# A two-layer hybrid backbone on Trainium2: the 32x32 inverses of the gated DeltaNet laid out by VectorE transposes instead of DMA, with other fill amounts and buffers

## The chip, the cores and the metric

One core of one Trainium2 chip runs the kernel. The metric is the device time of one execution in microseconds; smaller is better. A profiled execution gives the trace that the rows below come from.

## The reference, cut to what matters

The model has two layers over 512 latent tokens and 256 context tokens, 1024 wide. A layer normalises and modulates the stream, projects it once, and feeds three parallel mixers: a Conformer convolution, a neighbourhood attention, and a bidirectional gated DeltaNet (GDN). Their outputs are merged through sigmoid gates, and a gated ConvFFN follows. The change is in the GDN. Per head, direction and chunk of 64 tokens it solves a unit lower triangular system:

```python
lmat = jnp.where(strict, jnp.einsum("bhnid,bhnjd->bhnij", kb, k) * decay, 0.0)
rhs = jnp.concatenate([v * beta, kb * jnp.exp(g)[..., None]], axis=-1)
sol = lax.linalg.triangular_solve(lmat, rhs, left_side=True, lower=True, unit_diagonal=True)
```

The GDN has four heads of width 128. The kernel solves by the explicit inverse of blocks of 128 tokens, and needs four rounds of inverses in all: two layers times two pairs of heads. The text calls them L0/0, L0/1, L1/0 and L1/1.

## The kernel before

**Fills.** The GDN core is a long chain of small steps that would leave TensorE idle. So independent work is kept in a queue of generators (neighbourhood-attention projections `na`, convolution projections `pjl` and `pjc`, merge gates), and `fill(us)` (L426) issues as many of its matmuls as a nominal time asks for. The table `FILL` (L33) gives the amounts at each place of the core. A scheduler then places all instructions on the engines' queues; it may move fill matmuls ahead of steps that stand earlier in the code, and each engine runs its queue in order. What the core does not use up of the queue is issued later in the layer.

**Weight units.** Each queued projection loads a 128x1024 weight block on SP's queue into `raw`, ScalarE casts it to `whi` (L131), VectorE subtracts `wlo<-raw,whi` (L132), and TensorE multiplies with `whi` and `wlo` in turn. So a TensorE matmul that needs a `wlo` waits for whatever stands ahead of that subtraction on VectorE.

**The core.** `gdn_core` (L884) makes, for each of two heads and two directions, a decay `D` (VectorE L900, ScalarE exponential L902), products `kk` and `qk` on TensorE, and from them `E` (L912) and `A` (L924) on VectorE. Then it calls `gdn_inverse`, loads keys and values (`tk`) and runs the state chain, which begins with `ch` (L965).

**The inverse.** `gdn_inverse` (L1021) inverts 24 blocks of 128x128 with 32x32 diagonal blocks. It writes the diagonal blocks of `E` to DRAM and reads them back so that a block lies along one partition (L1031 to L1035; 48 partitions for each direction, the second one reversed by a copy). 31 substitution steps of two VectorE operations each follow (L1041, L1043), on 112 partitions. `fill(sub)` stands behind them. Two ScalarE copies and one VectorE copy arrange the result (L1046 to L1048), DMAs write it to DRAM (L1050, L1051), and eight loads bring it back with a block's rows along partitions: `Td`, and the diagonal of `E` (L1058, L1059). TensorE then builds the off-diagonal 32x32 products, `iy` (L1069, 48 matmuls) and `it` and `ir` (L1080, L1082, 72 matmuls), and the 64x64 products `iy` (L1101) and `ir` (L1110), with copies out of PSUM by ScalarE and VectorE between them and the fills `y32`, `t32`, `y64` and `t64`. A trace shows each of these small matmuls as two records. The tiles `D`, `Eb`, `Tt`, `Tf` and the key loads `tk` share a ring of three buffers.

**Convolution taps.** After marked instructions (`self.marks`) the scheduler may start the taps `ca` (L519) of the convolution on VectorE; they are many and short, and fill VectorE's gaps.

Of the kernel before, what the change touches and what calls it, by code (L numbers as in the profile page):

```python
# [9 lines left out]
F32 = mybir.dt.float32  # L10
# [54 lines left out]
class Net:  # L65
# [277 lines left out]
    def layer(self, l):  # L343
# [540 lines left out]
    def gdn_core(self, pr):  # L884
# [6 lines left out]
        for hh in range(2):  # L891
            h = 2 * pr + hh
            Ds = []
            for d in range(2):
                D = gp.tile([128, 1024], F32, tag="D", name="D", bufs=3)[:, 0:768].rearrange("p (t c) -> p t c", c=128)
                r0 = 24 * d + 6 * h
                nc.sync.dma_start(D.rearrange("p t c -> p (t c)"),
                                  self.d_row[r0:r0 + 6].rearrange("a b -> (a b)").unsqueeze(0).to_broadcast([128, 768]))
                for t in range(6):
                    V.scalar_tensor_tensor(D[:, t, :], D[:, t, :], self.G[:, 4 * d + h, t:t + 1], mk[d],  # L900
                                           ALU.subtract, ALU.min)
                S.activation(D, D, AF.Exp)  # L902
                Ds.append(D)
            for t0, t1 in ((2, 6), (0, 2)):
# [17 lines left out]
                for d in range(2):  # L922
# [4 lines left out]
        self.gdn_inverse(E)  # L927

        tk = [gp.tile([128, 1024], F32, tag="D", name=f"tk{i}", bufs=3) for i in range(3)]
# [67 lines left out]
        for hh in range(2):  # L997
            h = 2 * pr + hh
            o = oa[hh]
            sg = gp.tile([128, 6, 128], F32, tag=("Td", "TA")[hh], name="sgr")  # L1000
# [20 lines left out]
    def gdn_inverse(self, E):  # L1021

        nc, V, S, T, gp = self.nc, self.nc.vector, self.nc.scalar, self.nc.tensor, self.gp
        de, dt, dR = self.d_e
        Eb = gp.tile([128, 1024], F32, tag="D", name="Eb", bufs=3)
        Tt = gp.tile([128, 1024], F32, tag="D", name="Tt", bufs=3)
        Tf = gp.tile([128, 1024], F32, tag="D", name="Tf", bufs=3)
        Tm = gp.tile([128, 768], F32, tag="Y", name="Tm")
        nc.gpsimd.memset(Eb[32:64], 0.0)
# [6 lines left out]
        Mv = Eb.rearrange("p (j i) -> p j i", i=32)  # L1036
        Tv = Tt.rearrange("p (i c) -> p i c", c=32)
        for j in range(31):
            n, m = 31 - j, j + 1
            tm = Tm[0:112, 0:n * m].rearrange("p (a b) -> p a b", b=m)  # L1040
            V.tensor_tensor(tm, Mv[0:112, j, j + 1:32].unsqueeze(2).to_broadcast([112, n, m]),  # L1041
                            Tv[0:112, j, 0:m].unsqueeze(1).to_broadcast([112, n, m]), ALU.mult)
            i = V.tensor_tensor(Tv[0:112, j + 1:32, 0:m], Tv[0:112, j + 1:32, 0:m], tm, ALU.subtract)  # L1043
        self.marks.append(i.ins)
        self.fill(FILL[self.l]["sub"])
        S.copy(Mv[0:48], Tv[0:48].rearrange("p i c -> p c i"))  # L1046
        S.copy(Mv[64:112], Tv[64:112].rearrange("p i c -> p c i")[:, ::-1, ::-1])
        V.tensor_copy(Tf[64:112], Tt[64:112, ::-1])  # L1048
        for d, (Rs, Ts) in enumerate(((Eb[0:48], Tt[0:48]), (Eb[64:112], Tf[64:112]))):
            nc.sync.dma_start(dR[:, 12 * d:12 * d + 12, :], Rs)  # L1050
            nc.sync.dma_start(dt[:, 12 * d:12 * d + 12, :], Ts)  # L1051
        Td = gp.tile([128, 24, 32], F32, tag="Td", name="Td")
        TA = gp.tile([128, 12, 64], F32, tag="TA", name="TA")
        nc.gpsimd.memset(TA, 0.0)
        for b in range(4):
            q = slice(32 * b, 32 * b + 32)
            d = b // 2
# [17 lines left out]
        tb, rb = self.bank("it"), self.bank("ir")
        for u in range(12):
            for d in range(2):
                for s, t in prs[d]:
                    if s // 2 == d:
                        T.matmul(tb[32 * t:32 * t + 32, 32 * u:32 * u + 32], blk(t, 12 * d + u, t), Yq(t, u),  # L1080
                                 start=True, stop=True)
                    T.matmul(rb[32 * s:32 * s + 32, 32 * u:32 * u + 32], Yq(t, u), blk(t, 12 * d + u, t),  # L1082
                             start=True, stop=True)
        self.fill(FILL[self.l]["t32"])
        v = lambda x: x.rearrange("p (u c) -> p u c", c=32)
        S.copy(TA[32:64, :, 0:32], v(tb[32:64, 0:384]))
        S.copy(TA[64:96, :, 32:64], v(tb[64:96, 0:384]))
        for d in range(2):
            for s, t in prs[d]:
                V.tensor_copy(E[32 * s:32 * s + 32, 12 * d:12 * d + 12, 32 * t:32 * t + 32], v(rb[32 * s:32 * s + 32, 0:384]))  # L1090
# [4 lines left out]
        ybs, rbs = [], []  # L1095
        for hh in range(2):
            yb = self.bank("iy2")
            for u in range(6 * hh, 6 * hh + 6):
                for d in range(2):
                    s, t = st(d)  # L1100
                    T.matmul(yb[t, 64 * (u - 6 * hh):64 * (u - 6 * hh) + 64], E[s, 12 * d + u, t], TA[s, u, :],  # L1101
                             start=True, stop=True)
            S.activation(Y2[:, 6 * hh:6 * hh + 6, :], w(yb[:, 0:384]), AF.Copy, scale=-1.0)
        self.fill(FILL[self.l]["y64"])
        for hh in range(2):
            rb = self.bank("ir2")
            for u in range(6 * hh, 6 * hh + 6):
                for d in range(2):
                    s, t = st(d)
                    T.matmul(rb[s, 64 * (u - 6 * hh):64 * (u - 6 * hh) + 64], Y2[t, u, :], E[t, 12 * d + u, t],  # L1110
                             start=True, stop=True)
# [430 lines left out]
```

## Time and profile before

| | us |
|---|---|
| median of 3 runs | 2592.03 |
| lowest and highest of them | 2590.8, 2603.91 |
| the profiled execution | 2597.05 |
| its span in the trace | 2595.3 |
| TensorE busy | 2492.7 |
| VectorE busy | 1851.3 |
| ScalarE busy | 1067.5 |
| GpSimd busy | 8.4 |

The profiled execution is 1.75 us longer than its span and 5.0 us above the median. The mean granted clock of TensorE over the span is 0.984 of full speed. TensorE is busy for 96% of the span, so its queue sets the end: idle time of TensorE, and time in which it runs at the lower clock, are what an edit can add or take away, so long as the number of matmuls stays the same.

### The profile page before, as it was taken

Reading aid. Unit: us, or ns where it says so; the run is one execution under the profiler, and the core shown is the slowest. Engines: PE = TensorE matmul, PEld = TensorE weight load, DVE = VectorE, ACT = ScalarE, POOL = GpSimd, SP = SyncE. Lnnn points to the kernel's source line nnn. Section 1 sums busy time; section 2 is a strip of 40 time slices with the busy share of each in tenths; the row PEclk is TensorE's granted clock in tenths of the full one; section 3 lists DMA queues with packets and bytes.
Section 4 is the critical chain, followed back from the end, with each engine's and each line's share of the span. In section 5 each row is a group of like instructions: output and inputs, shape, how many; then the busy total and the mean of one; then the engine's idle time right before and its main releaser. Section 6 shows DMA issues by size and latency. Waiting matters only on the chain. (4 is left out here: it accounts for less than half of the span.)

```text
span 2595.3 us, 42261 instructions
## 1 busy us (share of the span) xinstructions
PE 2492.7 (96%) x16079; PEld 2156.4 (83%) x16079; DVE 1851.3 (71%) x4138; ACT 1067.5 (41%) x2159; POOL 8.4 (0%) x32
## 2 busy tenths in 40 slices
PE   6999999989999999999999999998989999999999
PEld 4889898977778888888888898887877778888887
DVE  6676478789678988776656477776768977755463
ACT  4564342445332344223223345634344543533242
POOL 0000000000000000000000000000000000000000
PEclk9999999999999999999999989998999999999999
DMA  7224434253458553443442342343446375333332
GB/s 253 91 76 138 130 98 142 94 186 107 153 184 267 182 173 123 123 159 116 147 135 87 110 142 96 120 135 112 147 124 213 101 245 188 128 93 98 97 98 89
DMA packets 207275, 356.75 MB, mean 137 GB/s; under 512 B 54832, under 2 KB 103200, under 8 KB 206944
## 3 DMA queue, kind: packets, MB, share of 16 engines
q1 hardware_dynamic: 182176, 320.97, 39.2%
q10 hardware_dynamic: 24896, 33.09, 3.6%
q8 instruction: 126, 2.06, 0.3%
q14 instruction: 77, 0.63, 0.1%
HBM read 297.31 MB, written 56.68 MB: 136 GB/s over the span
## 5 line engine op out<-in xcount | busy, mean ns | idle before, releaser
L132 DVE TENSOR_TENSOR wlo<-raw,whi 128x1024 fp32r<-128x1024 f32 (+2 forms) x319 | 385.4, 1209 | 295.2 <-ACT whi L131 291.8
L131 ACT CAST whi<-raw 128x1024 fp32r<-128x1024 f32 (+2 forms) x319 | 331.9, 1041 | 619.5 <-PE dn L150 198.3
L150 PE MATMUL upl<-hl,whi 128*128 128x512 f32 (+1 forms) x728 | 281.2, 388 | 3.9 <-ACT whi L131 2.3
L150 PE MATMUL upl<-hl,wlo 128*128 128x512 f32 (+1 forms) x728 | 281.0, 387 | 0.2 <-DVE wlo L132 0.2
L150 PE MATMUL upl<-ol,whi 128*128 128x512 f32 (+1 forms) x728 | 281.0, 387 | 0.0
L519 DVE SCALAR_TENSOR_TENSOR ca<-yp,caw,ca 128x783 f32<-128x783 f32 (+1 forms) x240 | 213.0, 888 | 6.4 <-ACT ca L512 3.7
L448 PE MATMUL pjl<-hl,whi 128*128 128x512 f32 x512 | 209.4, 409 | 7.6 <-ACT whi L131 7.6
L448 PE MATMUL pjl<-hl,wlo 128*128 128x512 f32 x512 | 205.5, 402 | 0.8 <-DVE wlo L132 0.7
L448 PE MATMUL pjl<-ol,whi 128*128 128x512 f32 x512 | 205.5, 401 | 0.0
L150 PEld LDWEIGHTS upl<-hl,whi 128*128 128x128 f32 x728 | 136.7, 188 | 33.1 <-ACT whi L131 2.5
L150 PEld LDWEIGHTS upl<-hl,wlo 128*128 128x128 f32 x728 | 136.7, 188 | 29.4 <-DVE wlo L132 0.4
L150 PEld LDWEIGHTS upl<-ol,whi 128*128 128x128 f32 x728 | 136.7, 188 | 29.4
L150 PE MATMUL dn<-fhl,whi 128*128 128x512 f32 x352 | 138.6, 395 | 0.6 <-DVE xml L1406 0.6
L150 PE MATMUL dn<-fll,whi 128*128 128x512 f32 x352 | 139.0, 395 | 0.0
L150 PE MATMUL dn<-fhl,wlo 128*128 128x512 f32 x352 | 139.0, 395 | 0.0
L448 PEld LDWEIGHTS pjl<-hl,whi 128*128 128x128 f32 x512 | 97.4, 190 | 29.0 <-ACT whi L131 9.7
L448 PEld LDWEIGHTS pjl<-hl,wlo 128*128 128x128 f32 x512 | 97.1, 190 | 21.0 <-DVE wlo L132 1.4
L245 DVE CUSTOM_DVE_ANT_1 aj<-at,crows,par 128x512 f32<-128x512 f32 x128 | 93.1, 747 | 29.5 <-DMA at<-ada_t 18.3
L448 PEld LDWEIGHTS pjl<-ol,whi 128*128 128x128 f32 x512 | 97.5, 190 | 19.0 <-issue 0.5
L584 PE MATMUL na<-wlo,hl 128*128 128x256 f32 x384 | 109.6, 285 | 0.6 <-DVE wlo L132 0.6
L584 PE MATMUL na<-whi,hl 128*128 128x256 f32 x384 | 109.8, 286 | 0.0
L584 PE MATMUL na<-whi,ol 128*128 128x256 f32 x384 | 109.8, 286 | 0.0
(405 smaller groups left out, 6457.5 us busy)
## 6 DMA issues: line engine op xcount, KB each, us to landing
raw<-w_b SPq DMA_DIRECT2D x88, 512.0 KB
raw<-f_up SPq DMA_DIRECT2D x88, 512.0 KB
at<-ada_t SPq DMA_DIRECT2D x160, 256.0 KB
raw<-w_o SPq DMA_DIRECT2D x32, 512.0 KB
raw<-f_dn SPq DMA_DIRECT2D x32, 448.0 KB
raw<-w_a SPq DMA_DIRECT2D x24, 512.0 KB
mg<-mge ACTq DMA_DIRECT2D x48, 256.0 KB
raw<-w_br SPq DMA_DIRECT2D x24, 512.0 KB
```

The source lines that it names most:

```text
L131: self.nc.scalar.copy(hi[:, :n], r[:, :n])
L132: self.split = self.nc.vector.tensor_sub(lo[:, :n], r[:, :n], hi[:, :n]).ins
L150: self.nc.tensor.matmul(o, wk[a], x[k][b], start=(k == 0 and i == 0), stop=(k == n - 1 and i == 2))
L245: V.tensor_tensor_reduce(p, w, self.crows[:, r, 4 * h:4 * h + 4], 1.0, m if h else self.p(l, "adab")[:, t:t + 1], ALU.mult, ALU.add, accum ...
L448: self.nc.tensor.matmul(o, wk[a], x[k][b], start=(k == 0 and i == 0), stop=(k == n - 1 and i == 2))
L519: nc.vector.scalar_tensor_tensor(a, y[:, k:k + n], w[:, 31 * c + k:31 * c + k + 1], a, ALU.mult, ALU.add)
L584: self.nc.tensor.matmul(ps[:, :256], x[k][a], wk[b], start=(k == 0 and j == 0), stop=(k == 7 and j == 2))
```

## The change

1. The four inverses no longer go through DRAM. VectorE transposes 32x32 squares instead: the diagonal squares of `E` go into `Db` (second direction by VectorE transposes, first direction by ScalarE copies), `Z` is the transpose of `Db`, the substitution runs on `Z` and `W` on 128 partitions, and two more transposes give `X` and `Yt`. GpSimd sets `W` to the identity.
2. The 32x32 products read `X` and `Yt` directly, with a step of 32 elements, and the copies into `TA` (ScalarE) and into the diagonal of `E` (VectorE) read them with the same step.
3. Each stage of products is cut into two halves of six blocks. `behind()` keeps a half in its place on TensorE's queue, and `wait()` puts a fill of 0.9 between halves.
4. `FILL`: `sub` goes from 37.6 to 47 and 34 (first and second pair of layer 0) and from 38.3 to 50 and 36 (layer 1); `y32`, `t32` and `y64` go.
5. The ring of `D` has five buffers; the new tiles and the key loads `tk` share it. `sgr` gets a buffer of its own in place of `Td`'s.

```diff
-FILL = (dict(e=3.5, sub=37.6, y32=1.6, t32=2.5, y64=1.3, t64=1.0, ...),
-        dict(e=4.1, sub=38.3, y32=1.0, t32=2.5, y64=1.69, t64=1.7, ...))
+FILL = (dict(e=3.5, sub=(47.0, 34.0), inv=0.9, t64=1.0, ...),
+        dict(e=4.1, sub=(50.0, 36.0), inv=0.9, t64=1.7, ...))
...
+    def behind(self):
+        eng = self.nc.tensor.engine
+        last = next((i for i in reversed(self.nc.cur_bb.bb.instructions) if i.engine == eng), None)
+        return self.tc.issue_after(last) if last is not None else ExitStack()
...
-        for b in range(4):
-            nc.sync.dma_start(de[b].rearrange("u (j i) -> j u i", i=32), E[32 * b:32 * b + 32, :, 32 * b:32 * b + 32])
-        nc.sync.dma_start(Eb[0:48], de[:, 0:12, :])
-        nc.sync.dma_start(Tf[64:112], de[:, 12:24, :])
-        V.tensor_copy(Eb[64:112], Tf[64:112, ::-1])
-        nc.sync.dma_start(Tt[0:112], self.A["eye32"][0:112])
+        nc.gpsimd.memset(cube(Db)[:, :, 24:32], 0.0)
+        nc.gpsimd.memset(W, 0.0)
+        nc.gpsimd.memset(W[:, ::33], 1.0)
+        for q in qs:
+            V.transpose(cube(Db)[q, :, 12:24].rearrange("p i u -> p u i"), E[q, 12:24, q])
+            S.copy(cube(Db)[q, :, 0:12].rearrange("p i u -> p u i"), E[q, 0:12, q])
+        V.transpose(Z, Db)
...
-            V.tensor_tensor(tm, Mv[0:112, j, j + 1:32].unsqueeze(2).to_broadcast([112, n, m]),
+            V.tensor_tensor(tm, Zv[:, j + 1:32, j].unsqueeze(2).to_broadcast([128, n, m]),
...
-        self.fill(FILL[self.l]["sub"])
...
-            nc.sync.dma_start(Td[q], dt[b].rearrange("u (j i) -> j u i", i=32))
-            nc.sync.dma_start(E[q, :, q], dR[b].rearrange("u (j i) -> j u i", i=32))
-            S.copy(TA[q, :, 32 * (b % 2):32 * (b % 2) + 32], Td[q, 12 * d:12 * d + 12, :])
+        self.fill(FILL[self.l]["sub"][pr])
+        X, Yt = sq("X"), sq("Yt")
+        V.transpose(X, W)
+        V.transpose(cube(Yt), Wv.rearrange("p i c -> p c i"))
+        inv, ivt = (cube(Yt), cube(X)), (cube(X), cube(Yt))
...
+        for u0, u1 in halves:
+            yb = self.bank("iy")
+            with self.behind():
...
+                            T.matmul(yb[32 * t:32 * t + 32, 32 * (u - u0):32 * (u - u0) + 32], blk(s, 12 * d + u, t),
+                                     inv[d][qs[s], :, 12 * d + u], start=True, stop=True)
+            S.activation(Y1[:, 32 * u0:32 * u1], yb[:, 0:192], AF.Copy, scale=-1.0)
+            wait()
+        for b, q in enumerate(qs):
+            d = b // 2
+            S.copy(TA[q, :, 32 * (b % 2):32 * (b % 2) + 32], inv[d][q, :, 12 * d:12 * d + 12].rearrange("p i u -> p u i"))
+            for d in range(2):
+                us = slice(12 * d, 12 * d + 12)
+                V.tensor_copy(E[q, us, q], ivt[d][q, :, us].rearrange("p i u -> p u i"))
```

The next two listings are VectorE's queue in L0/0, around the end of `E` and `A`, of before and then of the changed kernel. `nrm` is a small reduction of an `na` unit; the `wlo` is that of the first projection `pjl` behind the last `qk`.

```order
L900 SCALAR_TENSOR_TENSOR D<-D,G,km 128x128 x6
L592 TENSOR_REDUCE nrm<-nsq 128x4 x2
L132 TENSOR_TENSOR wlo<-raw,whi 128x1024
L900 SCALAR_TENSOR_TENSOR D<-D,G,km 128x128 x6
L912 SCALAR_TENSOR_TENSOR E<-kk,beta,D 128x128 x8
L924 TENSOR_TENSOR A<-qk,D 128x512 x2
L912 SCALAR_TENSOR_TENSOR E<-kk,beta,D 128x128 x4
L924 TENSOR_TENSOR A<-qk,D 128x256 x2
L592 TENSOR_REDUCE nrm<-nsq 128x4 x2
L132 TENSOR_TENSOR wlo<-raw,whi 128x1024
```

```order
L917 SCALAR_TENSOR_TENSOR E<-kk,beta,D 128x128 x8
L929 TENSOR_TENSOR A<-qk,D 128x512 x2
L917 SCALAR_TENSOR_TENSOR E<-kk,beta,D 128x128 x4
L929 TENSOR_TENSOR A<-qk,D 128x256 x2
L1040 STREAM_TRANSPOSE Db<-E 32x12x32 x4
L597 TENSOR_REDUCE nrm<-nsq 128x4
L1042 STREAM_TRANSPOSE Z<-Db 128x1024
L597 TENSOR_REDUCE nrm<-nsq 128x4
L1047 TENSOR_TENSOR Tm<-Z,W 128x31
L597 TENSOR_REDUCE nrm<-nsq 128x4
L1049 TENSOR_TENSOR W<-W,Tm 128x31
L132 TENSOR_TENSOR wlo<-raw,whi 128x1024
```

The subtraction `wlo` stood between the two groups of `D`; in the changed kernel the twelve `D` operations run together, and it stands behind `E`, `A`, five transposes and the first substitution step.

On the same engine in L1/0, the place that answers to it, before and then after; here the `wlo` belongs to an `na` unit.

```order
L900 SCALAR_TENSOR_TENSOR D<-D,G,km 128x128 x6
L592 TENSOR_REDUCE nrm<-nsq 128x4
L132 TENSOR_TENSOR wlo<-raw,whi 128x1024
L900 SCALAR_TENSOR_TENSOR D<-D,G,km 128x128 x6
L912 SCALAR_TENSOR_TENSOR E<-kk,beta,D 128x128 x8
```

```order
L917 SCALAR_TENSOR_TENSOR E<-kk,beta,D 128x128 x8
L929 TENSOR_TENSOR A<-qk,D 128x512 x2
L917 SCALAR_TENSOR_TENSOR E<-kk,beta,D 128x128 x4
L597 TENSOR_REDUCE nrm<-nsq 128x4
L1040 STREAM_TRANSPOSE Db<-E 32x12x32 x4
L132 TENSOR_TENSOR wlo<-raw,whi 128x1024
```

It has moved in the same way, behind `E` and four transposes.

VectorE's queue in L0/0 at the end of the substitution, before and then after. The copies `E<-ir` are those out of PSUM between the 32x32 and the 64x64 products.

```order
L1043 TENSOR_TENSOR Tt<-Tt,Tm 112x31
L1048 COPY Tf<-Tt 48x1024
L132 TENSOR_TENSOR wlo<-raw,whi 128x1024 x2
L592 TENSOR_REDUCE nrm<-nsq 128x4 x6
L1090 COPY E<-ir 32x12x32 x4
```

```order
L1053 STREAM_TRANSPOSE X<-W 128x1024
L132 TENSOR_TENSOR wlo<-raw,whi 128x1024
L1054 STREAM_TRANSPOSE Yt<-W 128x1024
L1089 COPY E<-X 32x12x32
L1089 COPY E<-Yt 32x12x32
...
L1089 COPY E<-Yt 32x12x32
L132 TENSOR_TENSOR wlo<-raw,whi 128x1024
L493 SCALAR_TENSOR_TENSOR th<-th,pjl 128x512
L493 SCALAR_TENSOR_TENSOR th<-th,pjc 128x256
L132 TENSOR_TENSOR wlo<-raw,whi 128x1024
L1105 COPY E<-ir 32x6x32 x8
```

Eight copies with strided reads now stand ahead of the `wlo` of the last projection that TensorE runs before its first `iy`. On TensorE's queue the work between the last `qk` and the first `iy` of L0/0 was 66.3 us by the pace of its matmuls in the trace (0.119 us from one `na` to the next, 0.236 for a `pjl`, 0.117 for a `pjc`); now it is 76 `na`, 96 `pjl` and 96 `pjc`, which is 42.9 us. In L0/1, L1/0 and L1/1 it goes from 65.4, 60.0 and 64.8 us to 39.2, 48.2 and 45.0 us.

## Rows read from the trace of the kernel before

**Rows 1.** The page, busy us of an engine (share of the span), instructions.

```profile
PE 2492.7 (96%) x16079; PEld 2156.4 (83%) x16079; DVE 1851.3 (71%) x4138; ACT 1067.5 (41%) x2159; POOL 8.4 (0%) x32
```

**Rows 2.** Waits of PE, whole span: what for, us in total, times, longest.

```profile
PE iy L1069 <- DMA Td<-e: 11.6, 5, 4.2
PE pjl L448 <- ACT whi L131: 7.6, 5, 2.6
PE it L1080 <- issue: 4.0, 1, 4.0
PE ir L1082 <- issue: 3.4, 3, 1.7
PE iy L1069 <- issue: 2.2, 1, 2.2
```

**Rows 3.** Four stretches: length, busy of PE, PEld, DVE, ACT, POOL, PE clock, DMA.

```profile
230.00:325.00 95.00, 89.76 (x910) 82.63 (x908) 48.89 (x118) 32.16 (x57) 0.00 (x0) 0.98 0.45 134
376.00:462.00 86.00, 78.63 (x809) 72.85 (x807) 66.71 (x138) 27.05 (x45) 0.00 (x0) 0.92 0.45 129
1690.00:1776.00 86.00, 72.15 (x771) 66.72 (x769) 56.03 (x129) 30.72 (x54) 0.95 (x1) 0.88 0.52 151
1827.00:1917.00 90.00, 82.75 (x726) 70.93 (x724) 58.03 (x123) 29.08 (x43) 0.15 (x2) 0.96 0.52 155
```

**Rows 4.** The same view of stretches at the lower clock inside them.

```profile
301.60:305.00 3.40, 3.40 (x19) 3.40 (x18) 0.00 (x0) 0.34 (x1) 0.00 (x0) 0.51 0.78 150
...
451.80:462.00 10.20, 6.37 (x159) 6.26 (x159) 5.01 (x8) 3.48 (x8) 0.00 (x0) 0.50 0.36 117
...
1759.10:1776.20 17.10, 10.19 (x337) 9.38 (x338) 3.48 (x7) 6.76 (x14) 0.00 (x0) 0.50 0.70 193
```

**Rows 5.** Timeline of DVE, L0/0: start, us, operation, count, idle before.

```profile
230.82 1.21 DVE L132 TENSOR_TENSOR wlo<-raw,whi 128x1024 fp32r<-128x1024 f32 x1
...
238.35 0.75 DVE L924 TENSOR_TENSOR A<-qk,D 128x256 f32<-128x256 f32 x2
239.01 0.73 DVE L592 TENSOR_REDUCE nrm<-nsq 128x4 f32<-128x256 f32 x2
```

**Rows 6.** Timeline of PE, L0/0: last qk, then the first use of that wlo.

```profile
229.36 0.60 PE L920 MATMUL qk<-qT,kT 128*128 128x128 f32 x4
...
233.87 0.40 PE L448 MATMUL pjl<-hl,wlo 128*128 128x512 f32 x1
```

**Rows 7.** Timeline of DVE, L1/0: the wlo, and the last E.

```profile
1691.93 1.22 DVE L132 TENSOR_TENSOR wlo<-raw,whi 128x1024 fp32r<-128x1024 f32 x1
...
1698.25 1.12 DVE L912 SCALAR_TENSOR_TENSOR E<-kk,beta,D 128x128 f32<-128x128 f32 x4
```

**Rows 8.** Timeline of PE, L1/0: the first use of that wlo.

```profile
1693.33 0.28 PE L584 MATMUL na<-wlo,hc 128*128 128x256 f32 x1
```

**Rows 9.** Timeline of DVE, L0/0: first and last of 62 substitution operations.

```profile
257.75 0.18 DVE L1041 TENSOR_TENSOR Tm<-Eb,Tt 112x31 f32<-112x31 f32 x1
...
285.04 0.19 DVE L1043 TENSOR_TENSOR Tt<-Tt,Tm 112x31 f32<-112x31 f32 x1
```

**Rows 10.** Instructions by line: count, least/mean/most ns, first and last start.

```profile
L131 ACT CAST whi<-raw x319: 941/1051/1111, 25.5 to 2574.3; 128x1024 fp32r<-128x1024 f32 x141, 128x896 fp32r<-128x896 f32 x16, 128x1088 fp32r<-128x1088 f32 x3
L1046 ACT COPY Eb<-Tt x4: 2077/2120/2154, 285.3 to 1877.4; 48x1024 f32<-48x1024 f32 x4
L1048 DVE COPY Tf<-Tt x4: 691/692/692, 285.3 to 1878.0; 48x1024 f32<-48x1024 f32 x4
L1090 DVE COPY E<-ir x16: 546/553/566, 320.0 to 1913.2; 32x384 f32<-32x384 f32 x16
```

**Rows 11.** Timeline of PE: the 32x32 products in L0/0 and L1/0.

```profile
300.96 0.21 PE L1069 MATMUL iy<-Td,E 32*32 32x32 f32 x2 [2.17 <-issue]
...
315.11 0.97 PE L1069 MATMUL iy<-Td,E 32*32 32x32 f32 x90
...
1761.86 1.48 PE L1069 MATMUL iy<-Td,E 32*32 32x32 f32 x90 [0.80 <-DMA Td<-e]
```

More of the change, by code (lines that the diff above doesn't have):

```diff
@@ L926, in gdn_core @@
                                     Ds[d][:, t0:t1, :], ALU.mult)
-        self.gdn_inverse(E)
-        tk = [gp.tile([128, 1024], F32, tag="D", name=f"tk{i}", bufs=3) for i in range(3)]
+        self.gdn_inverse(E, pr)
+        tk = [gp.tile([128, 1024], F32, tag="D", name=f"tk{i}", bufs=5) for i in range(3)]
         for j, (kind, hh) in enumerate((("v", 0), ("k", 0), ("v", 1), ("k", 1))):
@@ L999, in gdn_core @@
             o = oa[hh]
-            sg = gp.tile([128, 6, 128], F32, tag=("Td", "TA")[hh], name="sgr")
+            sg = gp.tile([128, 6, 128], F32, tag=("sg", "TA")[hh], name="sgr")
             nc.sync.dma_start(sg[:, c0:6, :], self.d_sg[128 * c0:, 128 * h:128 * h + 128]
@@ L1019, in gdn_core, with gdn_inverse @@
                 nc.scalar.dma_start(self.d_yc[h][:, self.sl(s)], ev[:, :n])
-    def gdn_inverse(self, E):
+    def gdn_inverse(self, E, pr):
         nc, V, S, T, gp = self.nc, self.nc.vector, self.nc.scalar, self.nc.tensor, self.gp
[L1024 to L1027, printed above, removed]
+        sq = lambda name: gp.tile([128, 1024], F32, tag="D", name=name, bufs=5)
+        cube = lambda t: t.rearrange("p (a b) -> p a b", b=32)
+        qs = [slice(32 * b, 32 * b + 32) for b in range(4)]
+        Db, Z, W = sq("Db"), sq("Z"), sq("W")
@@ L1044, in gdn_inverse @@
         self.marks.append(i.ins)
-        self.fill(FILL[self.l]["sub"])
[L1046 to L1052, printed above, removed]
+        self.fill(FILL[self.l]["sub"][pr])
@@ L1062, in gdn_inverse @@
         prs = (((0, 1), (2, 3)), ((1, 0), (3, 2)))
         Y = gp.tile([128, 12, 64], F32, tag="Y", name="Y")
+        Y1 = Y.rearrange("p a b -> p (a b)")[:, 0:384]
         blk = lambda q, u, c: E[32 * q:32 * q + 32, u, 32 * c:32 * c + 32]
-        yb = self.bank("iy")
-        for u in range(12):
+        dia = lambda t, d, u: ivt[d][qs[t], :, 12 * d + u]
+        Yq = lambda t, u: Y1[32 * t:32 * t + 32, 32 * u:32 * u + 32]
+        v = lambda x: x.rearrange("p (u c) -> p u c", c=32)
+        halves = [(6 * hh, 6 * hh + 6) for hh in range(2)]
@@ new lines, in wait @@
+        def wait():
+            with self.behind():
+                self.fill(FILL[self.l]["inv"])
+        for u0, u1 in halves:
+            yb = self.bank("iy")
+            with self.behind():
+                for u in range(u0, u1):
+                    for d in range(2):
+                        for s, t in prs[d]:
+                            T.matmul(yb[32 * t:32 * t + 32, 32 * (u - u0):32 * (u - u0) + 32], blk(s, 12 * d + u, t),
+                                     inv[d][qs[s], :, 12 * d + u], start=True, stop=True)
+            S.activation(Y1[:, 32 * u0:32 * u1], yb[:, 0:192], AF.Copy, scale=-1.0)
+            wait()
@@ new lines, in gdn_inverse @@
+        for b, q in enumerate(qs):
+            d = b // 2
+            S.copy(TA[q, :, 32 * (b % 2):32 * (b % 2) + 32], inv[d][q, :, 12 * d:12 * d + 12].rearrange("p i u -> p u i"))
+            for d in range(2):
+                us = slice(12 * d, 12 * d + 12)
+                V.tensor_copy(E[q, us, q], ivt[d][q, :, us].rearrange("p i u -> p u i"))
+        for u0, u1 in halves:
+            tb, rb = self.bank("it"), self.bank("ir")
+            with self.behind():
+                for u in range(u0, u1):
+                    c = 32 * (u - u0)
+                    for d in range(2):
+                        for s, t in prs[d]:
+                            if s // 2 == d:
+                                T.matmul(tb[32 * t:32 * t + 32, c:c + 32], dia(t, d, u), Yq(t, u),
+                                         start=True, stop=True)
+                            T.matmul(rb[32 * s:32 * s + 32, c:c + 32], Yq(t, u), dia(t, d, u), start=True, stop=True)
+            S.copy(TA[32:64, u0:u1, 0:32], v(tb[32:64, 0:192]))
+            S.copy(TA[64:96, u0:u1, 32:64], v(tb[64:96, 0:192]))
@@ L1076, in gdn_inverse @@
[L1076 to L1090, printed above, removed]
+                    V.tensor_copy(E[32 * s:32 * s + 32, 12 * d + u0:12 * d + u1, 32 * t:32 * t + 32],
+                                  v(rb[32 * s:32 * s + 32, 0:192]))
@@ L1092, in gdn_inverse @@
+            wait()
         Y2 = gp.tile([128, 12, 64], F32, tag="Y", name="Y2")
@@ L1094, in gdn_inverse @@
         w = lambda x: x.rearrange("p (u c) -> p u c", c=64)
-        ybs, rbs = [], []
-        for hh in range(2):
+        for u0, u1 in halves:
             yb = self.bank("iy2")
[L1098 to L1105, printed above, removed]
-            rb = self.bank("ir2")
[L1107 to L1111, printed above, removed]
+            with self.behind():
+                for u in range(u0, u1):
+                    for d in range(2):
+                        s, t = st(d)
+                        T.matmul(yb[t, 64 * (u - u0):64 * (u - u0) + 64], E[s, 12 * d + u, t], TA[s, u, :],
+                                 start=True, stop=True)
+            S.activation(Y2[:, u0:u1, :], w(yb[:, 0:384]), AF.Copy, scale=-1.0)
+            wait()
+        for u0, u1 in halves:
+            rb = self.bank("ir2")
+            with self.behind():
+                for u in range(u0, u1):
+                    for d in range(2):
+                        s, t = st(d)
+                        T.matmul(rb[s, 64 * (u - u0):64 * (u - u0) + 64], Y2[t, u, :], E[t, 12 * d + u, t],
+                                 start=True, stop=True)
             for d in range(2):
                 s, t = st(d)
-                V.tensor_copy(E[s, 12 * d + 6 * hh:12 * d + 6 * hh + 6, t], w(rb[s, 0:384]))
+                V.tensor_copy(E[s, 12 * d + u0:12 * d + u1, t], w(rb[s, 0:384]))
         self.fill(FILL[self.l]["t64"])
```

27 lines of the change are left out of this document (7 added, 20 removed).

## Prediction

> **What bounds the kernel now.** First the busy times of the page: TensorE works for 2492.7 us [rows 1] of a span of 2595.3, so the end moves only if its idle time, its clock or its order moves. Then the list of what TensorE waits for: 11.6 us of `iy` waiting for the `Td` loads are the one wait that the DMA hops cause directly; three rows of 4.0, 3.4 and 2.2 us, 9.6 together, name no releaser, only "issue"; and 7.6 us are projections waiting for a `whi` cast, about 5.1 of it inside the four stretches [rows 2]. Then the stretches from the last `qk` to the first `ch`. TensorE's idle time there is the length less its busy time [rows 3]: 95.00 - 89.76 = 5.24, 86.00 - 78.63 = 7.37, 86.00 - 72.15 = 13.85 and 90.00 - 82.75 = 7.25, in sum **33.7 us**. Last the granted clock. Seven pieces of the stretches run at 0.50 or 0.51, that is 1.2 instead of 2.4 GHz; three are shown, the other four are 3.4 us each with TensorE busy throughout [rows 4]. What is done at half speed takes twice as long, so half of the busy time is lost: (5 x 3.40 + 6.37 + 10.19) / 2 = **16.8 us**. It comes after a wait each time: the 90 `iy` records take 0.97 us in L0/0 and 1.48 us in L1/0, where the `Td` waits come first [rows 11]. Together 50.5 us, or 2% of the time, is the most that the change can give back; the rest of the program is the same work in the same order.
>
> **What the change removes.** The `Td` waits (11.6 us) go with the loads. The DMA hops on both sides of the substitution go: in L0/0 `E` ends near 238.4 and the first substitution starts at 257.75 [rows 9], 19 us of hops, copies and `wlo`s. In their place stand four small transposes and one of 128x1024. Neither is in the trace. The nearest contiguous VectorE copy of 1024 elements takes 0.69 us, a `wlo` of 1024 takes 1.21 [rows 5, 10], so 0.26 to 0.55 us for each small one (the 384-element copy out of PSUM is 0.553) and 0.7 to 1.2 for a large one; I take 0.4 and 0.95, between two near ends. So the chain from `E` to the substitution shrinks from 19 to 4 or 5 us, and that behind it, from the last subtraction at 285.2 to the first `iy` at 300.96 [rows 9, 11], from 16 to 3 or 4. In exchange the work laid in front of `iy` is 20 to 26 us shorter in three inverses and 12 in L1/0 (listings of the queues). The result arrives when TensorE does: in L0/0 about 241 + 27.5 (62 operations as now, [rows 9]) + 3 = 272 to 275, against TensorE at 230 + 42.9 = 273 without any stall. The `Td` waits become 0 to 2 us, and I take 2 for all four.
>
> **What it moves, L0/0.** This is the term that decides. The `wlo` of the first projection ends at 232.03 today, and TensorE uses it at 233.87 without waiting [rows 5, 6]. TensorE's queue up to there is the same in the changed kernel, but on VectorE the `wlo` now stands behind `D`, `E`, `A`, the transposes and the first step. `A` ends at 239.10 today [rows 5]; without the `wlo` and two `nrm` ahead of it that is 237.3. Behind it come four small transposes (1.0 to 2.2), one large (0.7 to 1.2), three `nrm` at 0.37 (1.1; two take 0.73 in [rows 5]), two short operations (0.4) and the `wlo` itself (1.21): it ends at 241.7 to 243.4. TensorE stands still for 7.8 to 9.5 us, since its queue is in order and the whole projection and all fills stand behind the waiting matmul; I take **8.5**. Nothing covers it.
>
> **L1/0.** The same: the `wlo` at 1691.93, first used at 1693.33 [rows 7, 8]. The last `E` ends at 1699.37 today, 1697.7 without the `wlo` and one `nrm`; then `nrm`, four transposes and the `wlo`: 1700.3 to 1701.5, less 1693.33 is 7.0 to 8.2 us; I take **7.5**. In L0/1 and L1/1 no `wlo` changes its place in this way.
>
> **Behind the substitution.** Eight copies of `E` from `X` and `Yt` stand ahead of the `wlo` of the last projection before `iy` in L0/0, and ahead of a `wlo` in L1/0 with convolution taps. A contiguous copy of 384 would be 0.26, one out of PSUM is 0.55 [rows 10]. Reading with a step of 32 may double it: ScalarE's rearranging copy takes 2.12 us for 1024 elements against 1.04 for the contiguous cast [rows 10]. So eight copies take 2 to 9 us. In L0/0 TensorE arrives about when `Yt` is done, and waits 2 to 8.6 us; I take 3.5, near the lower end, since the price of a VectorE copy has a row and its doubling has one on another engine only. In L1/0 some 10 us of slack leave 0 to 6; I take 2. In L0/1 the second half of the 64x64 stage can wait for copies out of PSUM behind taps, 0 to 6 us; I take 2.
>
> **The products.** The "issue" gaps have no cause in the profile; they may go with the dense blocks being cut up, or stay: 0 to 9.6, I take 5. `whi` waits stay, but one of 2.6 us falls into a stall: 3. The waits between halves are now filled: 1. Strided operands may slow the small matmuls: from nothing to twice the 0.97 us of `iy` and about 1.5 of `it` and `ir`, so 0 to 2.5 us for an inverse and 0 to 10 in all; I take 4, below the middle, because only ScalarE's row speaks for a doubling. The substitution reads one factor with the same step; L0/0 and L1/0 have room for it.
>
> The Trainium skill has a rule on this: its page "SBUF — State Buffer", section "Door 1: The DMA port swizzle", says that an access which steps to a new 16-byte line each time pays, so that fp32 may step by four elements for free. A step of 32 would then be slow on every engine; ScalarE's 2.12 us agrees with it. By the rule the sum would take the upper ends of these terms, which is the slower rival below.
>
> **Sum.** Idle after: 2 + 8.5 + 7.5 + 3.5 + 2 + 2 + 5 + 3 + 1 = 34.5 us, as much as the 33.7 now. The lower clock follows waits: after the wait of 2.17 us at 300.96 the clock is at 0.51 for 3.40 us [rows 4, 11], which costs 3.4 / 2 = 1.7 us. Four such dips (6.8) and one as long as that at 451.80 (10.2 / 2 = 5.1) are 12 us, against 16.8. With 4 us for the stride the loss is 50.5, the same as now. The gain on the DMA side is given back by the two stalls. I round to 2 us less, for the SP queue, on which weight loads no longer queue behind inverse loads: 2597.05 - 2 = 2595 for a run like the profiled one, which is 5.0 us above the median; so **2590 us** against the median of 2592.03.
>
> The skill's page "VectorE: DVE Perf Modes", section "The three transpose paths", gives 311 ns for a 128x128 bf16 transpose on VectorE. As an estimate from that, eight of them for 1024 columns would take 2.5 us, and the stall in L0/0 would be 1.3 us longer than with my upper end. No run here shows it yet.
>
> **Rivals.**
>
> *Faster: the stalls are all that is left.* If both `wlo` stalls come at their lower ends (7.8 + 7.0), strides cost nothing, the late `wlo`s find room (0), and the cut-up stages lose the "issue" gaps but 2 us, then with 3 for `whi` and four dips (6.8) the loss is 26.6: 24 us less, **2568 us**. For it: the clear waits at the products [rows 2] do lose their cause. Against it: the 9.6 us have no named cause, and the two stalls have rows.
>
> *Faster: the stalls do not appear* because VectorE reaches the `wlo` early or TensorE later than I read: 16 us and two dips of 3.4 to 5 us less than in the sum, about 22 us, **2568 us** again. Against it: VectorE cannot begin the `wlo` before `A` is done, 3.4 us after TensorE wants it, even with transposes for nothing.
>
> *Slower: strided reads double.* The place is the work right behind `Yt`: matmuls 10 us instead of 4, late `wlo`s 8.6 + 6 instead of 5.5, bank wait 5 instead of 2, stalls at their upper ends (1.7 more), and three more dips (5): 25 us more, **2615 us**; if half of it comes, 2603. It decides for slower by over 0.5% from about 15 us on, that is with copies of 0.9 us and matmuls at 1.7 times their time. For it: 2.12 against 1.04 us [rows 10]. Against it: VectorE and TensorE have no such row.
>
> *The change does not do what it says:* `iy` still waits, for `Yt` instead of `Td` (3 us in each inverse), and the "issue" gaps all stay. That is 10 + 5 us more than the sum with two dips on top, near 2605; it lies at the edge of no change.
>
> **How the numbers follow.** A measurement can tell about 0.5% (13 us) from no change. No change within it: 0.42, 2579 to 2605, time 2590. Faster: 0.22 for the first rival and 0.13 for the second, 0.35. Slower: 0.17 for the strides, 0.06 for waits that stay, 0.23. The likeliest case alone gives 2579 to 2605; the range for 8 in 10 reaches into the rivals, 2562 to 2611.
>
> **What would show it.** In the trace after: a wait of TensorE on `wlo` of 7 to 9 us near 234 and near 1693, with lower clock behind it; no wait of `iy` on a DMA; `iy` near 285 instead of 301; transposes of 128x1024 at 0.7 to 1.2 us; copies `E<-X` at 0.3 to 0.6 us; `iy` records at full clock at 0.97 us for some 90. If the waits on `wlo` are missing, I have misread the queues, and the time is near 2568. If copies `E<-X` take over 0.9 us, the slower rival holds.

## The result

The changed kernel takes 2615.93 us (median of 5 runs, 2613.34 to 2621.94), against 2592.59 us for the kernel before (5 runs). The ratio is **1.0093, with a 95% interval of 1.0072 to 1.0114**: slower by some 24 us. The forecast was 2590 us and no change, in a range that ended at 2611. It was wrong.

The page of the changed kernel, engine by engine (busy us, share, instructions), answers to [rows 1]:

```profile
PE 2491.3 (95%) x16079; PEld 2151.7 (82%) x16079; DVE 1892.6 (72%) x4206; ACT 1070.5 (41%) x2179; POOL 10.2 (0%) x40
```

The span is 2620.1 us. TensorE works as long as before; its idle time rose from 2595.3 - 2492.7 = 102.6 to 2620.1 - 2491.3 = 128.8 us. These 26.2 us, less 1.4 us of busy time, are the 24.8 us by which the span grew. VectorE has 41 us more to do.

What TensorE waits for in the changed kernel (us in total, times, longest), to be read beside [rows 2]:

```profile
PE lnT L541 <- DMA lnx<-ca: 21.5, 2, 20.7
...
PE na L589 <- DVE wlo L132: 12.8, 3, 8.9
PE pjl L453 <- DVE wlo L132: 12.2, 5, 10.1
...
PE PT L1248 <- DVE ls L1240: 9.9, 2, 5.2
...
PE pjl L453 <- ACT whi L131: 4.3, 5, 1.0
```

The waits on `Td` are gone, as they must be, and so are nearly all "issue" gaps at the products. The two `wlo` stalls that the prediction named are there. But the longest row is one that it did not name: `lnT`, the transposes that begin the normalisation of the convolution's output, wait 20.7 us for a load of `ca`, the result of the taps.

First the four stretches, from the last `qk` to the first `ch` (to within 2 us), in the columns of [rows 3]:

```profile
230.00:306.00 76.00, 63.17 (x676) 55.68 (x676) 58.34 (x142) 27.03 (x45) 0.00 (x0) 0.91 0.33 112
374.60:435.00 60.40, 57.64 (x707) 53.63 (x708) 58.11 (x127) 23.27 (x45) 0.00 (x0) 1.00 0.34 113
1698.00:1778.00 80.00, 67.89 (x757) 62.80 (x756) 67.95 (x153) 31.08 (x58) 0.36 (x2) 0.94 0.38 123
1843.00:1908.00 65.00, 62.54 (x596) 50.66 (x594) 62.16 (x121) 26.09 (x39) 0.00 (x0) 1.00 0.42 139
```

TensorE's idle time is 12.8, 2.8, 12.1 and 2.5 us, 30.2 in sum. Before it was 33.7. L0/1 and L1/1 have become nearly dense at full clock; L0/0 and L1/0 lose what the inverse saves to one wait each. VectorE, which was busy for 51 to 78% of these stretches, is now busy for 77 to 96% of them. Outside the stretches TensorE's idle time rose by 29.7 us, from 102.6 - 33.7 = 68.9 to 128.8 - 30.2 = 98.6. So what the kernel lost on balance, it lost outside.

L0/0 on VectorE and the matmul that waits (start, us, engine, line, operation, count, idle before and what ended it):

```profile
236.62 0.74 DVE L929 TENSOR_TENSOR A<-qk,D 128x256 f32<-128x256 f32 x2
237.28 3.29 DVE L1040 STREAM_TRANSPOSE Db<-E 32x384 f32<-32x384 f32 x4
240.60 0.42 DVE L597 TENSOR_REDUCE nrm<-nsq 128x4 f32<-128x256 f32 x1
240.94 1.23 DVE L1042 STREAM_TRANSPOSE Z<-Db 128x1024 f32<-128x1024 f32 x1
...
242.94 1.22 DVE L132 TENSOR_TENSOR wlo<-raw,whi 128x1024 fp32r<-128x1024 f32 x1
```

```profile
244.21 0.79 PE L453 MATMUL pjl<-hl,wlo 128*128 128x512 f32 x1 [10.05 <-DVE wlo L132]
```

`A` ends at 237.3, the four small transposes take 3.29 us, and the `wlo` is done at 244.16. TensorE has waited for it since 234.16. In L1/0 the same wait is 8.92 us:

```profile
1709.95 0.58 PE L589 MATMUL na<-wlo,hc 128*128 128x256 f32 x1 [8.92 <-DVE wlo L132]
```

Now the place that the prediction did not look at, in the attention of layer 1. TensorE, then VectorE:

```profile
2067.84 0.39 PE L453 MATMUL pjl<-hl,wlo 128*128 128x512 f32 x1
2088.96 1.09 PE L541 MATMUL lnT<-kc,lnx 128*128 128x128 f32 x4 [20.73 <-DMA lnx<-ca]
2089.97 0.81 PE L1233 MATMUL sc<-akT,aqT 64*128 64x256 f32 x2
```

```profile
2070.53 13.41 DVE L524 SCALAR_TENSOR_TENSOR ca<-yp,caw,ca 128x512 f32<-128x512 f32 x17
2090.08 0.70 DVE L545 BATCH_NORM_STATS2 bst<-lnT 128x6 f32<-128x512 f32 x1 [6.14 <-PE lnT L541]
```

TensorE has nothing to do from 2068.2 on, since `lnT` stands next on its queue and the taps are not done. VectorE runs the last 17 taps without a break until 2083.9; a store and a load follow. Attention scores (`sc`) stand behind `lnT`, and the first of them start right after it without a wait of their own. In the kernel before, the last `sc` is ahead of the first `lnT`:

```profile
2072.63 0.59 PE L1216 MATMUL sc<-akT,aqT 64*128 64x256 f32 x2
...
2081.53 0.60 PE L536 MATMUL lnT<-kc,lnx 128*128 128x128 f32 x4
```

The work of `lnT` is a unit at the end of the fill queue. The fills in the two inverses of layer 1 now ask for 50 + 36 + 12 x 0.9 = 96.8 us of it in place of 2 x 38.3 + 2 x (1.0 + 2.5 + 1.69) = 87.0. So the attention comes to the normalisation 9.8 us (nominal) of queue earlier, and 20 score matmuls (40 records) now stand behind the first `lnT`, where before none did.

### The profile page after: what moved, and what is told of

Read it like the earlier page. It is cut to its first block, busy times and chain, and to the rows that moved or that the text cites. A ratio compares the mean times of both kernels' runs of the same rounds, so it can differ in the third digit from the quotient of the medians.

```text
span 2620.1 us, 42235 instructions
## 1 busy us (share of the span) xinstructions
PE 2491.3 (95%) x16079; PEld 2151.7 (82%) x16079; DVE 1892.6 (72%) x4206; ACT 1070.5 (41%) x2179; POOL 10.2 (0%) x40
## 3 DMA queue, kind: packets, MB, share of 16 engines
q8 instruction: 127, 2.08, 0.3%
## 4 chain that ended last, share of the span: by engine, by line
PE 66%; DVE 14%; DMA 7%; ACT 2%; issue 2%; SPq 0%; DVEq 0%; ACTq 0%; POOL 0%; POOLq 0%
PE upl L150 19%; PE dn L150 11%; PE pjl L453 8%; PE upc L150 5%; PE mbl L150 4%; DVE ca L524 4%; PE na L589 3%; PE pjl L150 3%; PE pjc L453 2%; PE wo L150 2%; DVE wlo L132 2%; DMA mg<-mge 1%; PE og L623 1%; PE mbc L150 1%; DMA raw<-w_o 1%
## 5 line engine op out<-in xcount | busy, mean ns | idle before, releaser
L453 PE MATMUL pjl<-hl,whi 128*128 128x512 f32 x512 | 214.9, 420 | 4.3 <-ACT whi L131 4.3
```

The costliest lines, as they stand in the source:

```text
L453: self.nc.tensor.matmul(o, wk[a], x[k][b], start=(k == 0 and i == 0), stop=(k == n - 1 and i == 2))
```

## The experiments

Ratios are to the kernel before on the same chip; the changed kernel's is 1.0093.

**The ring.** Of the change's parts, which one moved the `wlo`? With three buffers the fourth `D` of a pair must wait until the first one is free, and a `wlo` comes in between; with five it need not.

```diff
-  ... tag="D", name="D", bufs=5)    (and the same in sq and tk)
+  ... tag="D", name="D", bufs=3)
```

> The changed kernel with a ring of three buffers for D, the new tiles and the key loads, in place of five. On VectorE's queue the wlo stands between the two last groups of D again. Theory (the ring moved the wlo, and TensorE's stalls of 10.05 us in L0/0 and 8.92 us in L1/0 come from that): both stalls are gone, total 2597 to 2604 us (12 to 19 less than the changed kernel); the wait of the transposes lnT on their load (20.7 us) stays above 10 us. Rival (the work in front of the block products is simply too short, and a stall moves from the wlo to the first iy): iy waits 5 to 9 us in both inverses, total within 6 us of 2616.

Measured: 2603.51 us, ratio 1.0022 (1.0003 to 1.0040), so 0.7% less than the changed kernel, about 18 us. The longest waits on a `wlo` are 1.6 us (`na`) and 1.0 us (`pjl`), and `iy` waits 0.8 us in all: the stalls did not move on. The wait of `lnT` is as long as it was:

```profile
PE na L589 <- DVE wlo L132: 3.0, 2, 1.6
...
PE pjl L453 <- DVE wlo L132: 2.2, 3, 1.0
```

```profile
2065.57 0.66 PE L541 MATMUL lnT<-kc,lnx 128*128 128x128 f32 x2 [20.69 <-DMA lnx<-ca]
```

The other half of the test puts the ring alone into the kernel before.

```diff
-  ... tag="D", ..., bufs=3)
+  ... tag="D", ..., bufs=5)         (D, Eb, Tt, Tf and tk of the kernel before)
```

> The kernel before with a ring of five buffers in place of three, and nothing else. On VectorE's queue the wlo in L0/0 and L1/0 moves behind all of D, E and A, as in the changed kernel, but no transposes stand between. Theory of the ring: TensorE waits 4 to 6 us for a wlo in L0/0 and in L1/0, which were 0 before; total 2600 to 2612. Rival (the earlier loads that five buffers allow make up for it): 2588 to 2596.

Measured: 2609.84 us, ratio 1.0049 (1.0028 to 1.0069). Two waits of the forecast size appear in a kernel that has no transposes:

```profile
238.61 0.79 PE L448 MATMUL pjl<-hl,wlo 128*128 128x512 f32 x1 [5.05 <-DVE wlo L132]
```

```profile
1703.07 0.58 PE L584 MATMUL na<-wlo,hc 128*128 128x256 f32 x1 [5.59 <-DVE wlo L132]
```

So the ring is the cause, and what the new inverse puts behind `E` only makes the wait longer, by some 5 and 3 us.

**The queue.** Two runs change nothing but an amount of fill. The first gives 9.8 us back ahead of the attention of layer 1 (ten fills of 0.98 less).

```diff
-  ... x=2.0, pre=2.08, att=1.41))
+  ... x=2.0, pre=1.1, att=1.41))
```

> The changed kernel with fills of 1.1 in place of 2.08 between the steps that prepare the attention of layer 1, so that by the first attention job about as much of the queue (10 us nominal) is used as before. On TensorE's queue no score matmul stands behind the first lnT, as before the change. Theory (the larger fills in the inverses use the queue up, so lnT comes before the taps are done): the wait of lnT falls from 20.7 to under 3 us, total 2596 to 2602. Rival (VectorE has some 11 us more to do in each inverse, so the taps end later in any case): the taps end near 2080 as now and lnT waits 8 us or more, total 2605 to 2612.

Measured: 2591.94 us, ratio 0.9986 (0.9968 to 1.0004), 1.1% less than the changed kernel. The waits of `lnT` are 0.5 us in all, and the time lies below the range said. Of the rival the tap times came true, but not the wait: the taps end at 2082.9, nearly as late as in the changed kernel, and the first `lnT` now stands behind the scores and starts at 2091.6. The last tap of the kernel before, then of e2, and the `lnT` of e2:

```profile
2072.16 0.74 DVE L519 SCALAR_TENSOR_TENSOR ca<-yp,caw,ca 128x512 f32<-128x512 f32 x1
```

```profile
2082.19 0.74 DVE L524 SCALAR_TENSOR_TENSOR ca<-yp,caw,ca 128x512 f32<-128x512 f32 x1
```

```profile
2091.60 0.60 PE L541 MATMUL lnT<-kc,lnx 128*128 128x128 f32 x4
```

Nor is it VectorE's added work that makes the taps late. The program hands them out with the attention's jobs, so they move with the attention. Its preparation ends with the transposes `aT` (ns of one as least, median and most; first and last start), here of the kernel before, the changed kernel and e2:

```profile
L1166 PE MATMUL aT<-kc,ax x88: 270/272/329, 531.1 to 1983.2; 128*128 128x128 f32 x88
```

```profile
L1184 PE MATMUL aT<-kc,ax x88: 270/273/421, 524.0 to 1993.7; 128*128 128x128 f32 x88
```

```profile
L1184 PE MATMUL aT<-kc,ax x88: 270/272/448, 524.7 to 1990.9; 128*128 128x128 f32 x88
```

From the last `aT` the taps take 89.7, 90.2 and 92.0 us in the three kernels, which is nearly the same. What moved is TensorE's arrival at the first `lnT`: 98.3, 74.5 and 100.7 us after that point. In the changed kernel 90.2 us, and 5.0 us for the store and the load, less 74.5 are the 20.7 us of the wait.

The second takes the 9.8 us from the kernel before.

```diff
-        dict(e=4.1, sub=38.3, ...
+        dict(e=4.1, sub=43.2, ...
```

> The kernel before with fills of 43.2 in place of 38.3 in both inverses of layer 1, and nothing else: 9.8 us more of the queue are used, as in the changed kernel. Sixteen score matmuls stand behind the first lnT on TensorE's queue. Theory of the used-up queue: TensorE comes to lnT near 2065, the taps end near 2073 as before, lnT waits 6 to 11 us, total 2597 to 2605. Rival (the taps' lateness alone makes the wait): lnT waits under 3 us, total 2588 to 2595.

Measured: 2624.14 us, ratio 1.0106 (1.0075 to 1.0137). One number of the table makes the kernel before as slow as the changed one. The same wait is there, with 16.4 of the some 27 us that are lost; the rest is in smaller waits and time at the lower clock, which were not added up. The wait is longer than expected, because the attention begins later (last `aT` at 1990.3) and the taps end at 2079.6 and not at 2073. That is 89.3 us behind the last `aT`, as in the other kernels; TensorE is there after 77.9 us:

```profile
L1166 PE MATMUL aT<-kc,ax x88: 270/272/445, 529.2 to 1990.3; 128*128 128x128 f32 x88
```

```profile
2075.69 3.90 DVE L519 SCALAR_TENSOR_TENSOR ca<-yp,caw,ca 128x512 f32<-128x512 f32 x5
```

```profile
2084.54 1.08 PE L536 MATMUL lnT<-kc,lnx 128*128 128x128 f32 x4 [16.39 <-DMA lnx<-ca]
```

**Both.** The changed kernel with both edits.

> The changed kernel with both edits: ring of three, and fills of 1.1 in place of 2.08 ahead of the attention of layer 1. If the two causes are separate and make up the loss, the gains add: 2578 to 2588, faster than the kernel before by 4 to 14 us, which is what the shorter chain of the inverse is worth. If VectorE's added work is what costs, it stays above 2592.

Measured: 2578.63 us, ratio **0.9933 (0.9908 to 0.9957)**, faster than the kernel before. The run was made a second time beside others:

> e4 once more, beside e9 on the same chip: 2572 to 2585, in the same ratio to the kernel before as in the first run (0.993).

Measured: 2577.70 us, ratio 0.9909 (0.9879 to 0.9940). The gains of e1 and e2 add: 0.7% and 1.1% from 1.0093 would be 0.992. The four stretches of e4:

```profile
230.00:294.00 64.00, 61.08 (x669) 53.74 (x668) 53.38 (x124) 25.12 (x42) 1.12 (x2) 0.97 0.38 120
362.70:424.20 61.50, 58.14 (x709) 54.00 (x710) 57.74 (x132) 23.51 (x46) 1.11 (x2) 1.00 0.35 117
1680.00:1751.80 71.80, 66.13 (x756) 60.94 (x756) 66.46 (x146) 30.40 (x57) 1.12 (x2) 1.00 0.40 131
1814.00:1881.00 67.00, 64.81 (x614) 52.87 (x612) 64.42 (x131) 26.88 (x41) 1.12 (x2) 1.00 0.41 137
```

Idle time of TensorE is 2.9, 3.4, 5.7 and 2.2 us, 14.1 in sum against 33.7 in [rows 3], and the clock is full in three of four. That is what the new inverse is worth: the transposes in place of the DMA hops, together with the cut-up products and the other fill amounts. No run takes the transposes apart from these.

Does it matter where the queue is given back?

```diff
-  sub=(50.0, 36.0), inv=0.9, t64=1.7, ...       (layer 1, ring of three)
+  sub=(45.1, 31.1), inv=0.9, t64=1.7, ...
```

> The changed kernel with a ring of three buffers, and in layer 1 fills behind the substitution of 45.1 and 31.1 in place of 50 and 36; the fills ahead of the attention stay at 2.08. It gives back the same 9.8 us of the queue at another place than e4. If only the amount of the queue that is left counts, the wait of lnT is under 3 us and the total is that of e4 (2575 to 2583) or up to 5 us more, as far as the first iy of layer 1 now waits. If the place counts, lnT still waits.

Measured: 2576.03 us, ratio 0.9923 (0.9898 to 0.9947), which cannot be told from e4; `lnT` waits 1.7 us in all. Of these two places either will do: the amount counts.

**The strides.** The prediction's slower rival. On top of e4 every step of 32 elements is taken away; the numbers that the inverse works on are then others. (That the time does not hang on the numbers is taken for granted here.)

```diff
-            V.transpose(cube(Db)[q, :, 12:24].rearrange("p i u -> p u i"), E[q, 12:24, q])
+            V.transpose(cube(Db)[q, 12:24, :], E[q, 12:24, q])
...
-        V.transpose(cube(Yt), Wv.rearrange("p i c -> p c i"))
+        V.transpose(Yt, W)
...
-        dia = lambda t, d, u: ivt[d][qs[t], :, 12 * d + u]
+        dia = lambda t, d, u: ivt[d][qs[t], 12 * d + u, :]
...
-                V.tensor_copy(E[q, us, q], ivt[d][q, :, us].rearrange("p i u -> p u i"))
+                V.tensor_copy(E[q, us, q], ivt[d][q, us, :])
```

> The kernel with ring of three and fills of 1.1 (e4), but every read and write of the new tiles with a step of 32 elements is made contiguous: the same number of elements, the wrong ones, so the inverse computed is another matrix. If strides are a price (the slower rival of the prediction): the copies of E fall from 0.51 to about 0.3 us, the second large transpose from 2.06 to 1.24, the products get shorter by a third or more, and the total falls by 5 to 12 us from e4's 2578.6. If strides are nearly free here: the total stays within 4 us of e4.

Measured: 2556.01 us, ratio 0.9846 (0.9829 to 0.9863), some 0.6 to 0.9% below e4: more than expected. The prices, as least, median and most ns of an instruction (the middle number in [rows 10] is a median too), first in e4, then in e5:

```profile
L1040 DVE STREAM_TRANSPOSE Db<-E x16: 822/882/895, 238.1 to 1820.3; 32x384 f32<-32x384 f32 x16
L1054 DVE STREAM_TRANSPOSE Yt<-W x4: 2005/2057/2090, 274.5 to 1855.5; 128x1024 f32<-128x1024 f32 x4
L1086 ACT COPY TA<-X x8: 849/905/929, 274.7 to 1855.5; 32x384 f32<-32x384 f32 x8
L1089 DVE COPY E<-X x16: 430/502/525, 276.5 to 1860.4; 32x384 f32<-32x384 f32 x16
L1080 PE MATMUL iy<-X,E x192: 218/228/230, 277.5 to 1864.5; 32*32 32x32 f32 x192
```

```profile
L1040 DVE STREAM_TRANSPOSE Db<-E x16: 555/569/575, 239.0 to 1811.0; 32x384 f32<-32x384 f32 x16
L1054 DVE STREAM_TRANSPOSE Yt<-W x4: 1202/1204/1235, 274.2 to 1846.0; 128x1024 f32<-128x1024 f32 x4
L1086 ACT COPY TA<-X x8: 507/510/511, 274.4 to 1845.5; 32x384 f32<-32x384 f32 x8
L1089 DVE COPY E<-X x16: 304/350/358, 275.3 to 1849.0; 32x384 f32<-32x384 f32 x16
L1080 PE MATMUL iy<-X,E x192: 191/191/212, 275.6 to 1854.3; 32*32 32x32 f32 x192
```

A step of 32 makes ScalarE's copies and VectorE's transposes slower by a factor of 1.5 to 1.8, VectorE's copies by 1.4, and a record of the small matmuls by 1.2. On VectorE that is 4 x 0.31 + 0.85 + 8 x 0.15 = 3.3 us for an inverse, 13 us for four, most of it in the chain from `E` to the first `iy`. TensorE's 32x32 products take 22.7 us of its busy time in e4 and 18.2 in e5, 4.5 less. How the whole gain of 16 to 22 us splits was not measured. One strided read costs nothing: the substitution reads `Z` with the step, and its 124 multiplications (`Tm<-Z,W`) take 42.41 us in e4 and 42.35 in e5.

In the changed kernel itself, with the same edit:

> The changed kernel itself (ring of five, all fills as they are), with contiguous reads and writes as in e5: the wrong elements, so another matrix is inverted; the time alone counts. If the strides cost there what they cost on top of e4 (22 us), they are a cause of its own in the changed kernel and the total is 2590 to 2600. If the wait for the wlo and the wait of lnT hide them, the gain is under 10 us: 2606 to 2616.

Measured: 2610.56 us, ratio 1.0047 (1.0029 to 1.0065), 0.46% less. The `lnT` wait (20.7 us) and the `wlo` stalls (9.1 and 7.9 us) stay:

```profile
PE lnT L541 <- DMA lnx<-ca: 21.8, 2, 20.7
...
PE pjl L453 <- DVE wlo L132: 9.9, 4, 9.1
PE na L589 <- DVE wlo L132: 8.6, 2, 7.9
```

So the strides are a third cause. By the ratios they cost some 12 us here, and the intervals leave room for 5 to 19. The time lies in the range of the second guess, though the gain is not clearly under 10 us.

Can they be had for less? The transposes behind the substitution can write with the step, so that all readers are contiguous; nothing else is computed.

```diff
-        V.transpose(X, W)
-        V.transpose(cube(Yt), Wv.rearrange("p i c -> p c i"))
+        V.transpose(cube(X).rearrange("p u i -> p i u"), Wv)
+        V.transpose(cube(Yt).rearrange("p u c -> p c u"), Wv.rearrange("p i c -> p c i"))
```

> e4 (ring of three, fills of 1.1), with the step of 32 elements taken once: the two large transposes behind the substitution write with it, so that X and Yt hold each block's rows contiguously, and the products, the copies into TA and the copies of E read contiguously. Nothing is computed otherwise. If e5's gain comes from what the readers of X and Yt pay: the copies of E take 0.35 us, the records of the products 0.19, the transposes 2 us or more each, and the total is 2562 to 2574. If it comes from the transposes themselves (Db and Yt), nothing is gained: 2575 to 2583.

Measured: 2574.25 us, ratio 0.9900 (0.9870 to 0.9929), beside e4's second run at 0.9909 on the same chip: the two cannot be told apart, to within some 0.4%. The copies of `E` fall to 0.35 us, but the transpose of `X` rises from 1.24 to 2.08 us, so on VectorE 8 x 0.15 us are gained and 0.9 lost.

**The fills between halves.**

```diff
-  inv=0.9
+  inv=0.0
```

> e4 without the fills between the halves of the block products (0 in place of 0.9). If the fills are what closes the gaps at the products: TensorE waits 0.5 to 1 us for a copy out of PSUM at each of some 20 places, the clock falls behind them, total 2588 to 2600. If the loads' removal alone closes them: total within 5 us of e4's 2578.6.

> e9 without the fills between the halves of the products. In e6 this edit moved nothing that can be told from noise. If it holds here too, the total is within 6 us of e9's; if the shorter copies make the fills needless, 3 to 8 us below e9.

Measured: e6 2575.69 us, ratio 0.9921 (0.9896 to 0.9947); e10 2580.79 us, ratio 0.9917 (0.9890 to 0.9943). Neither can be told from e4 or e9, though in e6 gaps named "issue" are back at the products, 2.9 and 1.3 us the longest. The two runs also give back queue, so they don't show that the gaps between halves are free, only that the two effects together are.

## Why the prediction was wrong

**What held.** The largest terms of the sum were there. The `wlo` stall was sized at 8.5 us in L0/0 and 7.5 in L1/0 and measured 10.05 and 8.92; both lie above the bounds, because four small transposes take 3.29 us and not 1.0 to 2.2. Their output is written with a step of 32, which I had counted for readers only; without it they take 0.57 us each (e5), 2.3 in all. The 4 us taken for strided operands of the products are 4.5 (e4 against e5). Idle time in the four stretches came to 30.2 us, against a sum of 34.5 and 33.7 before. `iy` starts at 288.7 in L0/0 (285 said). The "issue" gaps, of which I kept half, are all but gone. So inside the stretches the forecast erred by a few us, to the pessimistic side.

**The step that failed** stands in the first paragraph: "the rest of the program is the same work in the same order". It is the same work, but not in the same order. I counted what the larger fills bring in front of `iy`, and not what they take from the queue behind it. 9.8 us more were drawn in layer 1, a unit that waits for VectorE's taps came ahead of attention scores on TensorE's queue, and the wait is 20.73 us. The sum had nothing for it. e2 and e3 settle this: the amount alone takes the wait away from the changed kernel and puts it into the kernel before. With the wait gone, e2's ratio of 0.9986 is 2589 us beside the 2592.59 of the result, where the forecast had 2590. That it comes so near is partly luck, since the two `wlo` stalls are 3 us longer than taken and the "issue" gaps at the products some 4 us shorter. The order of TensorE's queue at `lnT`, which could be read before any run, was the view that I left out.

**The chances.** The slower rival had a time of 2615 us, nearly the one measured, but not for its reason. Its copies and late `wlo`s were to cost TensorE 14.6 us behind `Yt`; the longest such wait is 2.05 us, in L1/0. The strides did cost about 12 us in the changed kernel (e11); where they cost it was not taken apart, but the two `wlo` stalls have 2 us of it. The rule of the Trainium skill that I cited against the change (page "SBUF — State Buffer", section "Door 1: The DMA port swizzle": a step to a new 16-byte line costs each time) agrees with e5 in direction on all three engines; how much each pays, a factor of 1.2 to 1.8, is what the runs add. The substitution's read of `Z` is the exception (42.41 against 42.35 us). I had set the price of a strided VectorE copy between 0.26 and 1.1 us for 384 elements and took a value near the lower end. Measured are 0.50, and 0.35 without the step.

**The other estimate from a page.** By the Trainium skill's page "VectorE: DVE Perf Modes", section "The three transpose paths", I had estimated 2.5 us for a transpose of 1024 columns. Contiguous it takes 1.24 us, a little over the upper end of my bound from rows; strided 2.06.

Set against the changed kernel, the ring costs about 0.7%, the queue 1.1% and the strides about 0.5%. Without ring and queue effects the new inverse, with its cut-up products and fill amounts, gains 0.7 to 0.9% over the kernel before. What is not settled: smaller waits that differ between the two traces, such as `PT` on `ls` (9.9 us), have no run of their own. They stand at the start of the attention, 5.2 us in layer 0 and 4.8 in layer 1; e2 has only the first, and e4 has 0.9 us in all.

## What to carry to other kernels

Where a queue of filler work covers waits, an amount drawn earlier is missing later: look up on the bound engine's queue which unit now comes next at the end of the queue, and what that unit itself waits for. A larger ring of buffers also takes away waits that kept an order; compare the queues of every engine before and after, not only the lines that were edited. When a layout is chosen, count the step of the writes as well as of the reads, on each engine that touches it.

## What the runs showed of the hardware

- VectorE transposed a 128x1024 fp32 tile in 32x32 squares in 1.24 us when both sides were contiguous, as long as its subtraction `wlo` of the same size (1.22 us), and in 2.06 us with a step of 32 elements on one side; with it on both sides it took 2.13 us (`Yt` of e9), so the second side was nearly free.
- A strided read need not cost anything: VectorE's `Tm<-Z,W`, which reads `Z` with a step of 32 and uses each element for a row of products, took a median of 0.360 us in e4 and 0.359 without the step (e5).
- The clock of TensorE followed the long waits here too. The stretch ahead of the `lnT` wait, the wait and the one behind it (length, busy time of PE, PEld, DVE, ACT and POOL, clock, DMA):

```profile
2062.50:2068.30 5.80, 5.73 (x25) 4.40 (x24) 5.69 (x10) 1.28 (x4) 0.00 (x0) 1.00 0.47 158
2068.30:2089.00 20.70, 0.04 (x1) 0.07 (x2) 14.97 (x20) 0.79 (x1) 0.00 (x0) 0.60 0.15 51
2089.00:2096.00 7.00, 5.81 (x34) 3.88 (x35) 5.39 (x24) 2.52 (x6) 0.00 (x0) 0.72 0.10 28
```

  It was full before the wait. In the 7 us behind it TensorE was busy for 5.81 us at a mean of 0.72 of full speed, so part of the matmuls ran at 1.2 instead of 2.4 GHz.
